# A gated encoder layer: longer split-weight tiles, with the 1024 columns placed inside them by a byte offset

## The chip, the core and the metric

The kernel runs on one core of one Trainium2 chip. The metric is the device time in microseconds of one execution. Three runs of the kernel before gave 1268.78, 1269.10 and 1269.41 us, so the median is 1269.1 us. One further execution was profiled; its own time was 1268.47 us.

## The reference

The input is `x`, 512 tokens by 1024 features, in float32, and one layer is computed:

```
x = x + 1/2 * SwiGLU_1(RMSNorm(x))                 # 1024 -> 2816 -> 1024
h = RMSNorm(x);  [A | B | gates] = h @ w_in        # 1024 -> 4608 + 1536 + 2048
A: dilated sliding-window attention, 3 groups of 8 heads of 64
B: grouped-query attention, 8 query and 2 key heads of 128, rotary
mix = (sigmoid(gA) * (oA @ P_A) + sigmoid(gB) * (oB @ P_B)) @ w_out
x = x + mix
x = x + 1/2 * SwiGLU_2(RMSNorm(x));  output RMSNorm(x)
```

## The kernel before

**Split products.** Every large product is taken in three matmuls of a reduced float32 type. Each operand is split into a high part H, rounded, and a low part L, the rest; `mm3` (L235) issues H·H, H·L and L·H into one PSUM bank (L237, L238, L239). A matmul has a stationary operand of 128x128, which TensorE loads (the PEld rows of the profile), and a moving operand of 128 rows by 512 or 256 columns, which streams past it.

**Weights.** The weights come as 288 tiles of 128x1024 float32, in one fixed list (`self.order`). A tile is loaded into a raw tile (`wr`, `wa`, `ws` or `wt`), then `prep` (L207) makes its two halves: ScalarE casts raw into `wh` (L222), VectorE subtracts to get `wl` (L223). `wh` and `wl` have three buffers each in the pool `wb`; a fourth one, with tag `whx`, lies in whichever pool `wx` is open at the time, and is used in the seven-product stages, the down projections and the `wb` projection when the tile's number n has n % 4 == 3 (L211). `ring` (L159) hands the tiles out. PE runs its instructions in the order in which the program issues them; `weights` (L227) prepares as many tiles ahead as the rings allow.

**Who reads the tiles.** A tile feeds 24 matmuls of 512 columns, or 24 of 256 columns in the seven-product stages.

- `feat` and `pair` (first FFN tiles `w13a`, `w13b`, the gates `wg`, four `waq` tiles): stationary `wh`/`wl`, moving `hH`/`hL`, 512 columns.
- `strassen` (L289): seven products for two-by-two blocks, used for most of the up projections and for the query/key projection; stationary `wh`/`wl`, moving 256 columns of `hH`/`hL`, `TH`/`TL` or `TQH`/`TQL`. A step is one tile. The stages have 14, 28 and 21 tiles in the first FFN, 35 for query/key, and 21, 28 and 21 in the second FFN: 168 in all.
- `blocks` (down projections `w2a`, `w2b`, branch products `wab`, output product `wo`): stationary `wh`/`wl`, moving `gg`, `oH`, `qH` or `mH`, 512 columns. The last three tiles of `w2b` are read twice, with 256 columns each time (L567 to L572).
- `token` (value projections `wav` of three groups, four tiles each, and `wb`, 12 tiles): here the activations `hH`/`hL` are stationary and the tile moves, 512 columns at a time. For groups 1 and 2 of `wav` the stationary operand takes every fourth token, so its 128 columns lie 16 bytes apart.

During the attention stages the gate, `waq` and `wb` work is woven in between the attention's own short matmuls and transposes, some matmuls at a time (`weave`, L365).

**Where the tiles lie.** A tile has the same byte address in each partition. The addresses follow from the tile sizes in the order in which the pools are opened, and are those of the kernel as built. What matters below is the remainder of the first byte's address by 256; slices along a tile start at multiples of 512 bytes from there, except the strided ones, which start 4, 8 or 12 bytes later.

| tile | first bytes | remainder by 256 |
|---|---|---|
| `wh`, three buffers | 50080, 54176, 58272 | 160 |
| `wl`, three buffers | 62368, 66464, 70560 | 160 |
| `whx` in the FFNs, in the query/key stage | 120352, 144928 | 32 |
| `whx` while `wb` is projected | 160160 | 160 |
| `hH0` to `hL7` | 196576 to 227296, steps of 2048 | 224 |
| `TH`, `TL`, `TQH`, `TQL` | 171744, 184032, 83424, 99808 | 224 |
| `gg`, four buffers | 136864, 145056, 153248, 161440 | 160 |
| `oH0`, `qH`, `mH0`, `kH`, `vH` | 83360, 99744, 132512, 132512, 140704 | 160 |

The lines that the change touches are in `ring` and in the mixer, where `rope_tables` (L886) opens its tables in the pool `Bp`, which then serves as `wx` for the `wb` projection.

Of the kernel before, what the change touches and what calls it, by code (L numbers as in the profile page):

```python
# [12 lines left out]
F32R = mybir.dt.float32r  # L13
# [3 lines left out]
DRAM = bass.MemoryType.DRAM  # L17

BUFS = {"wr": 3, "wa": 3, "ws": 2, "wt": 4, "wh": 3, "whx": 1}
EARLY, EARLIER = 4, 6  # L20
GROUPS = {"a": (4, 8, 16, 22), "b": (2, 8, 16, 22)}
PAIRS = ((0, 0), (1, 0), (0, 1), (0, 2), (1, 1), (1, 2), (2, 0), (3, 0), (2, 1), (2, 2), (3, 1), (3, 2))
# [16 lines left out]
NF = 22  # L39
# [26 lines left out]
def f32(t):  # L66
    return t.bitcast(F32)


class Layer:  # L70
    def __init__(self, ctx, tc, a):
# [41 lines left out]
        self.cap = len(self.order)  # L113
        self.rings = {k: [] for k in BUFS}
        self.index = {it[:2]: n for n, it in enumerate(self.order)}
# [43 lines left out]
    def ring(self, tag, n, done, last):  # L159
        held, bufs = self.rings[tag], BUFS[tag]  # L160
        pool = self.wb if tag in ("wr", "wh") else self.wx
        if pool is None or (len(held) >= bufs and held[-bufs] >= done):
            return None
        held.append(last)
        if tag[:2] != "wh":
            return pool.tile([128, 1024], F32, tag=tag, name=tag, bufs=bufs)
        return tuple(pool.tile([128, 1024], F32R, tag=t, name=t, bufs=bufs) for t in ("wh", "wl"))

    @staticmethod
    def home(it):  # L170
# [834 lines left out]
    def mixer(self):  # L1005
# [7 lines left out]
        with tc.tile_pool(name="oA", bufs=1, reuse_waits="tile") as oa:  # L1013
# [25 lines left out]
            with tc.tile_pool(name="B", bufs=1, reuse_waits="tile") as bp:  # L1039
                self.qH = bp.tile([128, 8, T], F32R, name="qH")  # L1040
                self.qL = bp.tile([128, 8, T], F32R, name="qL")
                with tc.tile_pool(name="KV", bufs=1, reuse_waits="tile") as kv:
                    self.kH = kv.tile([128, 2, T], F32R, name="kH")
                    self.kL = kv.tile([128, 2, T], F32R, name="kL")
                    self.vH = kv.tile([128, 4, 256], F32R, name="vH")
                    self.vL = kv.tile([128, 4, 256], F32R, name="vL")
                    with tc.tile_pool(name="Bp", bufs=1, reuse_waits="tile") as b2:
                        self.rope_tables(b2)
                        self.wx = b2
                        self.until(fill, ("b", 0))  # L1050
                        self.weave(self.rope_t(0, 4, 4), fill)
                        self.until(fill, ("b", 1))
                        self.weave(self.rope_t(1, 6, 6), fill)
                        self.until(fill, ("b", 2))
                        self.weave(self.rope_t(2, 6, 4), fill)
                    self.wx = None
                    with tc.tile_pool(name="Ba", bufs=2, reuse_waits="tile") as pp:
                        self.weave(self.attn_b(pp), fill)
                for _ in fill:
                    pass  # L1060
                self.hctx.close()
                with tc.tile_pool(name="M", bufs=1, reuse_waits="tile") as mp:
                    mH = [mp.tile([128, T], F32R, name=f"mH{d}") for d in range(NK)]
                    mL = [mp.tile([128, T], F32R, name=f"mL{d}") for d in range(NK)]
                    m = {}

                    def gate(j):
                        z = mp.tile([128, T], F32, tag="z", name="zg", bufs=4)
                        nc.sync.dma_start(z, self.gate_d[j])
                        nc.scalar.activation(z, z, AF.Sigmoid, bias=self.par[:, G_BG + j:G_BG + j + 1])  # L1070
                        return z

                    def done_a(d, ps):
                        m[d] = mp.tile([128, T], F32, tag="ma", name="ma", bufs=2)
                        nc.vector.tensor_mul(m[d], ps, gate(d))

                    def done_b(d, ps):
                        z = gate(NK + d)
                        nc.vector.tensor_mul(z, ps, z)
                        nc.vector.tensor_add(z, z, m[d])  # L1080
                        nc.scalar.copy(mH[d], z)
                        nc.vector.tensor_sub(mL[d], z, f32(mH[d]))

                    def done_o(d, ps):
                        nc.vector.tensor_add(self.x[d], self.x[d], ps)
                        self.norm_h(d, G_FFN2)
                        self.norm_sq(d)

                    oa_p = list(zip(self.oH, self.oL))
                    ob_p = [(self.qH[:, k, :], self.qL[:, k, :]) for k in range(8)]  # L1090
                    rows = []
                    for d in range(NK):
                        rows += [(oa_p, lambda ps, d=d: done_a(d, ps)), (ob_p, lambda ps, d=d: done_b(d, ps))]
                    self.blocks("wab", rows)
                    self.open_h()
                    mm = list(zip(mH, mL))
                    self.blocks("wo", [(mm, lambda ps, d=d: done_o(d, ps)) for d in range(NK)])
# [132 lines left out]
```

## Time and profile before

| | |
|---|---|
| median of three runs | 1269.1 us |
| profiled execution, its own time | 1268.47 us |
| span of its profile | 1266.7 us |
| PE busy | 1254.0 us, 8002 matmul records |
| PE's weight loads (PEld) busy | 1113.0 us |
| VectorE (DVE) busy | 888.2 us |
| ScalarE (ACT) busy | 587.3 us |
| bytes moved by DMA | 181.91 MB |

A matmul's recorded time runs from its start to its modelled end, and consecutive matmuls overlap. What a matmul costs the stream is the distance from its start to the next one's. A view of busy time by stretches gives it: a stretch that begins at the first matmul of a stage and ends at the first of the next, divided by the number of weight loads in it (there is one for each matmul).

### The profile page before, as it was taken

Reading aid. Unit: us, or ns where it says so; the run is one execution under the profiler, and the core shown is the slowest. Engines: PE = TensorE matmul, PEld = TensorE weight load, DVE = VectorE, ACT = ScalarE, POOL = GpSimd, SP = SyncE. Lnnn points to the kernel's source line nnn. Section 1 sums busy time; section 2 is a strip of 40 time slices with the busy share of each in tenths; the row PEclk is TensorE's granted clock in tenths of the full one; section 3 lists DMA queues with packets and bytes.
Section 4 is the critical chain, followed back from the end, with each engine's and each line's share of the span. In section 5 each row is a group of like instructions: output and inputs, shape, how many; then the busy total and the mean of one; then the engine's idle time right before and its main releaser. Section 6 shows DMA issues by size and latency. Waiting matters only on the chain.

```text
span 1266.7 us, 19954 instructions
## 1 busy us (share of the span) xinstructions
PE 1254.0 (99%) x8002; PEld 1113.0 (88%) x8002; DVE 888.2 (70%) x1339; ACT 587.3 (46%) x867; POOL 118.6 (9%) x124
## 2 busy tenths in 40 slices
PE   9999999999999999999999999999999999999997
PEld 6897999899889999877888878888889989988996
DVE  7784688478784885766557898654677847875775
ACT  8551355145453443644234465543475415532553
POOL 1111100000210212100001100000301001100001
PEclk9999999999999999999999999999999999999998
DMA  9875777342484946532232310356737536744222
GB/s 289 232 190 168 190 193 193 98 102 68 136 227 136 240 122 245 167 107 91 84 105 84 117 50 26 118 163 191 227 93 185 172 100 183 186 148 116 57 78 67
DMA packets 85549, 181.91 MB, mean 144 GB/s; under 512 B 12480, under 2 KB 19024, under 8 KB 85456
## 3 DMA queue, kind: packets, MB, share of 16 engines
q1 hardware_dynamic: 67904, 140.74, 33.6%
q0 software_dynamic: 16832, 39.34, 15.3%
q8 instruction: 63, 1.03, 0.4%
q10 hardware_dynamic: 720, 0.55, 0.1%
q14 instruction: 30, 0.25, 0.1%
HBM read 168.98 MB, written 15.29 MB: 145 GB/s over the span
## 4 chain that ended last, share of the span: by engine, by line
PE 93%; DVE 3%; issue 1%; DMA 1%; ACT 1%; POOL 0%; SPq 0%; POOLq 0%; DVEq 0%
PE mm L237 24%; PE mm L239 24%; PE mm L238 23%; PE Y L237 3%; PE Y L239 3%; PE Y L238 3%; PE X L239 2%; PE X L237 2%; PE X L238 2%; PE S L790 1%; PE mm L841 1%; PE Tb L980 1%; PE T L859 1%; DVE wl L223 0%; PE Sb L237 0%
## 5 line engine op out<-in xcount | busy, mean ns | idle before, releaser
L222 ACT CAST wh<-wr 128x1024 fp32r<-128x1024 f32 x142 | 148.9, 1049 | 211.7 <-PE mm L238 139.6
L223 DVE TENSOR_TENSOR wl<-wr,wh 128x1024 fp32r<-128x1024 f32 x142 | 173.7, 1224 | 54.8 <-ACT wh L222 54.2
L237 PE MATMUL mm<-hH,wh 128*128 128x256 f32 (+1 forms) x600 | 200.4, 334 | 0.2
L239 PE MATMUL mm<-hH,wl 128*128 128x256 f32 (+1 forms) x600 | 196.1, 327 | 0.9 <-DVE wl L223 0.9
L238 PE MATMUL mm<-hL,wh 128*128 128x256 f32 (+1 forms) x600 | 195.9, 326 | 0.3 <-DVE hL L374 0.3
L237 PE MATMUL mm<-gg,wh 128*128 128x512 f32 (+1 forms) x376 | 142.3, 379 | 0.0
L239 PE MATMUL mm<-gg,wl 128*128 128x512 f32 (+1 forms) x376 | 141.8, 377 | 0.0
L238 PE MATMUL mm<-gg,wh 128*128 128x512 f32 (+1 forms) x376 | 141.8, 377 | 0.0
L237 PEld LDWEIGHTS mm<-hH,wh 128*128 128x128 f32 x600 | 112.8, 188 | 14.9 <-issue 3.2
L239 PEld LDWEIGHTS mm<-hH,wl 128*128 128x128 f32 x600 | 112.7, 188 | 12.2 <-DVE wl L223 1.3
L238 PEld LDWEIGHTS mm<-hL,wh 128*128 128x128 f32 x600 | 112.8, 188 | 10.6 <-DVE hL L374 1.1
L222 ACT CAST wh<-wa 128x1024 fp32r<-128x1024 f32 x48 | 50.4, 1051 | 100.0 <-PE mm L238 48.6
L505 DVE TENSOR_TENSOR u<-mm,R 128x512 f32<-128x512 f32 (+1 forms) x52 | 33.7, 649 | 82.9 <-PE mm L239 82.5
L223 DVE TENSOR_TENSOR wl<-wt,wh 128x1024 fp32r<-128x1024 f32 x48 | 58.7, 1224 | 36.6 <-ACT wh L222 35.6
L238 PE MATMUL mm<-TL,wh 128*128 128x256 f32 x304 | 84.0, 276 | 0.0
L239 PE MATMUL mm<-TH,wl 128*128 128x256 f32 x304 | 84.0, 276 | 0.0
L237 PE MATMUL mm<-TH,wh 128*128 128x256 f32 x304 | 84.0, 276 | 0.0
L237 PEld LDWEIGHTS mm<-gg,wh 128*128 128x128 f32 x376 | 70.8, 188 | 14.6 <-PE mm L239 0.9
L239 PEld LDWEIGHTS mm<-gg,wl 128*128 128x128 f32 x376 | 70.8, 188 | 13.4
L222 ACT CAST wh<-ws 128x1024 fp32r<-128x1024 f32 x48 | 50.5, 1052 | 68.9 <-PE mm L238 51.4
L238 PEld LDWEIGHTS mm<-gg,wh 128*128 128x128 f32 x376 | 70.8, 188 | 13.1
L223 DVE TENSOR_TENSOR wl<-wa,wh 128x1024 fp32r<-128x1024 f32 x48 | 58.6, 1221 | 30.0 <-ACT wh L222 29.9
(233 smaller groups left out, 3164.1 us busy)
## 6 DMA issues: line engine op xcount, KB each, us to landing
wr<-in_w2a SPq DMA_DIRECT2D x22, 512.0 KB, 3.4
wr<-in_w2b SPq DMA_DIRECT2D x22, 512.0 KB, 3.9
wt<-in_w13b SPq DMA_DIRECT2D x20, 512.0 KB, 4.1
wa<-in_w13b SPq DMA_DIRECT2D x20, 512.0 KB, 3.8
wt<-in_w13b POOLq DMA_DIRECT2D x20, 512.0 KB, 5.8
wt<-in_w13a SPq DMA_DIRECT2D x18, 512.0 KB, 3.5
wt<-in_w13a POOLq DMA_DIRECT2D x18, 512.0 KB, 6.2
wa<-in_w13a SPq DMA_DIRECT2D x18, 512.0 KB, 3.4
```

The costliest lines, as they stand in the source:

```text
L222: self.nc.scalar.copy(H, raw)
L223: self.nc.vector.tensor_sub(L, raw, f32(H))
L237: mm(out, lH, rH, start=start, stop=False, skip_group_check=more)
L238: mm(out, lH, rL, start=False, stop=False, skip_group_check=more)
L239: mm(out, lL, rH, start=False, stop=stop, skip_group_check=more)
L505: nc.vector.tensor_mul(u, ps, R)
L790: nc.tensor.matmul(*args, start=True, stop=True)
L841: nc.tensor.matmul(oc, v, p, start=st, stop=sp)
L859: nc.tensor.transpose(ps[:, 128 * b:128 * b + 128], P[h][:, c0 + 128 * b:c0 + 128 * b + 128], self.ident)
L980: nc.tensor.transpose(pt[:, 128 * j:128 * j + 128], P[h, j][:, 128 * k:128 * k + 128], self.ident)
```

## The change

The tiles `wh` and `wl`, of both tags, become 1088 elements wide, which is 4352 bytes, 17 times 256. The 1024 columns in use begin `at` elements into the tile, 0 to 63, so that their first byte has the remainder that the new function `offset` names for tile n:

- seven-product stages (`sw...`): 160 for even n, 32 for odd n
- `w2a`, `wab`, `wo` and `w2b` up to its tile 18: 160
- `w2b` from its tile 19 on (those read with 256 columns): 96
- all others (`w13a`, `w13b`, `wav`, `waq` outside the seven-product stage, `wg`, `wb`): 224

`BASE` is the remainder of the tiles' own first byte: 160 in `wb`, 32 for `whx`. So that this holds for `whx` in `Bp` too, `rope_tables` gets its pool with a 128-byte tile ahead of it. All other tiles move by whole multiples of 256 bytes.

```
+BASE = {"wh": 160, "whx": 32}
...
-        return tuple(pool.tile([128, 1024], F32R, tag=t, name=t, bufs=bufs) for t in ("wh", "wl"))
+        at = (self.offset(n) - BASE[tag]) % 256 // 4
+        return tuple(pool.tile([128, 1088], F32R, tag=t, name=t, bufs=bufs)[:, at:at + 1024] for t in ("wh", "wl"))
+
+    def offset(self, n):
+        name, key = self.order[n][:2]
+        if name[:2] == "sw":
+            return 160 - 128 * (n % 2)
+        if name == "w2b" and key >= (NF + GROUPS["b"][2]) // 2:
+            return 96
+        return 160 if name in ("w2a", "w2b", "wab", "wo") else 224
...
-                        self.rope_tables(b2)
+                        self.rope_tables(self.shifted(b2, 128))
```

## The prediction

> **What bounds the kernel now.** I read the page's totals first, then the waits of PE and ScalarE, then the busy time by stretches. The page:
>
> ```profile
> span 1266.7 us, 19954 instructions
> PE 1254.0 (99%) x8002; PEld 1113.0 (88%) x8002; DVE 888.2 (70%) x1339; ACT 587.3 (46%) x867; POOL 118.6 (9%) x124
> PE 93%; DVE 3%; issue 1%; DMA 1%; ACT 1%; POOL 0%; SPq 0%; POOLq 0%; DVEq 0%
> ```
>
> PE is busy for 1254.0 of 1266.7 us and holds 93% of the chain that ended last. Who waits for whom (engine, line, releaser; total us, times, longest):
>
> ```profile
> PE warm L1106 <- POOL R L94: 1.3, 1, 1.3
> PE rb L406 <- POOL r L391: 1.0, 1, 1.0
> PE mm L239 <- DVE wl L223: 0.9, 1, 0.9
> ACT wh L222 <- PE mm L238: 277.1, 123, 5.5
> ```
>
> The preparation of the weights waits for PE to free a buffer (277.1 us in 123 waits), and PE waited only once for a weight half, 0.9 us. So what a matmul takes off the stream comes off the time, and the question is how many nanoseconds each matmul takes. The stretches below begin and end at the first matmuls of tiles or stages; the columns are the stretch, its length, then busy us and instructions of PE and PEld.
>
> ```profile
> core 0: us, PE busy (x) PEld busy (x) DVE busy (x) ACT busy (x) POOL busy (x), PEclk, DMA share, GB/s
> 31.57:53.54 21.97, 21.97 (x98) 18.03 (x96) 16.98 (x22) 11.74 (x17) 3.65 (x3) 1.00 0.98 284
> 53.54:73.33 19.79, 19.79 (x169) 19.79 (x168) 14.63 (x14) 9.81 (x12) 3.58 (x3) 1.00 0.72 159
> 73.33:92.37 19.04, 19.04 (x170) 19.04 (x169) 16.17 (x17) 10.77 (x12) 1.20 (x1) 1.00 0.66 193
> 242.36:247.95 5.59, 5.59 (x26) 4.53 (x24) 2.52 (x3) 1.06 (x2) 0.00 (x0) 1.00 0.32 98
> 247.95:258.84 10.89, 10.89 (x49) 9.01 (x48) 6.26 (x7) 2.09 (x3) 1.18 (x1) 1.00 0.37 83
> 373.34:396.21 22.87, 22.87 (x98) 22.82 (x97) 6.24 (x7) 5.59 (x6) 0.31 (x1) 1.00 0.40 115
> 639.20:661.60 22.40, 22.40 (x97) 18.05 (x96) 15.65 (x55) 8.39 (x14) 1.41 (x2) 1.00 0.31 106
> 874.67:918.19 43.52, 43.52 (x194) 36.05 (x192) 26.65 (x29) 18.20 (x24) 12.58 (x9) 1.00 0.80 238
> 1237.39:1245.98 8.59, 8.59 (x73) 8.58 (x72) 5.86 (x11) 4.07 (x8) 1.95 (x2) 1.00 0.00 0
> ```
>
> PE is never idle in them and the granted clock is 1.00, yet the same shape of matmul has several prices. With 512 columns: 43.52/192 = 226.7 ns in `wo`, and 10.89/48 = 226.9 in two `w2a` tiles in `wh`; 21.97/96 = 228.9 in `feat`; 5.59/24 = 232.9 in a `w2a` tile that lies in `whx`; 22.40/96 = 233.3 in `token` on `wb`; 22.87/96 = 238.2 on the strided `wav` group. With 256 columns: 19.04/168 = 113.3, 19.79/168 = 117.8, and 8.59/72 = 119.3 at the end. 113.3 is half of 226.7; I take both as the floor of the stream.
>
> Put beside the table of addresses, the 512-column prices sort by d, the remainder of the operand to be loaded less that of the moving one. d = 0 (`wo`, `w2a` in `wh`) gives the floor; d = 192 (160 against 224, `feat`) 2.2 ns over it; d = 128 (32 against 160) 6.2; d = 64 (224 against 160, `token`) 6.7. That 256 is the period is seen in `gg` and `mH`: their addresses differ by 256 modulo 512, and both stand at the floor. The groups of instructions in such stretches say the same with recorded times, which are some 162 ns longer than the distance between starts (the first row from 874.7 to 918.1, the second from 242.4 to 247.9, the third from 639.3 to 661.5):
>
> ```profile
> L237 PE MATMUL mm<-mH,wh 128*128 128x512 f32 x64 | 24.9, 389 | 0.0
> L237 PE MATMUL mm<-gg,wh 128*128 128x512 f32 x8 | 3.2, 396 | 0.0
> L237 PE MATMUL mm<-wh,hH 128*128 128x512 f32 x32 | 12.7, 396 | 0.0
> ```
>
> **The change, term by term.** Nothing is issued that was not issued before, but for the byte position of operands. The casts and subtractions keep their 1024 columns; if another offset made each pair 0.1 us longer, it would lie in the 277.1 us for which ScalarE waits anyway (uncovered, 288 tiles would be 29 us). The 128-byte tile in `Bp` moves the rotary tables and 40 short transposes; cost zero.
>
> *(a) `w2a`/`w2b` tiles in `whx`, d from 128 to 0.* n % 4 == 3 falls on 11 of the tiles read with 512 columns: 11 x 24 x (232.9 - 226.9) = 1.58 us. I take 1.5. Bounds 0 and 1.6.
>
> *(b) `token` on contiguous columns, d from 64 to 0.* `wb` has 12 tiles, the first `wav` group 4: 16 x 24 x (233.3 - 226.7) = 2.5 us. Rotary transposes lie between some of them, and after an interruption the stream does not come back to the floor at once (see d), so I take 2.0. Bounds 0.8 and 2.5.
>
> *(c) `feat` in the FFNs, d from 192 to 0.* 8 + 4 tiles: 12 x 24 x 2.2 = 0.63 us; I take 0.5, bounds 0 and 0.6. The first eight tiles run while DMA is at a share of 0.98, so 0.3 of this could be given back as a wait for a weight half.
>
> *(d) `feat` woven into attention, 20 tiles, d from 192 to 0.* Here three to twelve matmuls run between transposes. The groups from 709 to 809.3, where `Sb` has d = 0 already and `feat` has d = 192:
>
> ```profile
> L237 PE MATMUL mm<-hH,wh 128*128 128x512 f32 x56 | 22.4, 399 | 0.0
> L239 PE MATMUL mm<-hH,wl 128*128 128x512 f32 x56 | 22.0, 393 | 0.0
> L238 PE MATMUL mm<-hL,wh 128*128 128x512 f32 x56 | 21.9, 391 | 0.0
> L237 PE MATMUL Sb<-kH,qH 128*128 128x512 f32 x32 | 12.8, 400 | 0.0
> L239 PE MATMUL Sb<-kH,qL 128*128 128x512 f32 x32 | 12.6, 394 | 0.0
> L238 PE MATMUL Sb<-kL,qH 128*128 128x512 f32 x32 | 12.5, 392 | 0.0
> ```
>
> Equal remainders buy nothing in so short a run: means of 395 (`Sb`) and 394 (`feat`), against 389 in the steady stretch. I take 0. Bounds: 480 x 3 ns = 1.4 us lost, if `feat` becomes like the slower `Sb` rows, and 480 x 5 = 2.4 gained, if it reaches 389.
>
> *(e) `token` on strided columns, two `wav` groups, 8 tiles, d from 64..76 to 0..12.* No row has a strided load near d = 0. The loads' recorded time in 373.4 to 396.1 (strided) and 349.1 to 373.3 (contiguous):
>
> ```profile
> L238 PEld LDWEIGHTS mm<-wl,hH 128*128 128x128 f32 x32 | 9.9, 310 | 0.0
> L238 PEld LDWEIGHTS mm<-wl,hH 128*128 128x128 f32 x32 | 6.0, 188 | 1.3
> ```
>
> The strided load is 122 ns longer, so it may itself set the 238.2 ns, and then the offset changes nothing; that is the nearest row, and I take 0. Bounds: 192 x (238.2 - 226.7) = 2.2 us gained; as much lost as (b) wins per matmul, 192 x 6.7 = 1.3.
>
> *(f) Seven-product stages, 168 tiles, 256 columns.* The moving remainder stays 224; the tiles' goes from 160, 160, 160, 32 to 160 and 32 in turn. The stages, and the second one again without its first tile:
>
> ```profile
> 53.54:92.37 38.83, 38.83 (x337) 38.83 (x336) 30.80 (x31) 20.58 (x24) 4.78 (x4) 1.00 0.69 175
> 138.69:214.96 76.27, 76.27 (x673) 76.26 (x672) 62.33 (x62) 41.65 (x47) 8.33 (x7) 1.00 0.75 192
> 141.52:214.96 73.44, 73.44 (x650) 73.44 (x649) 59.81 (x59) 40.62 (x46) 8.33 (x7) 1.00 0.74 194
> 258.84:316.07 57.23, 57.23 (x505) 57.23 (x504) 44.06 (x44) 30.94 (x35) 1.19 (x1) 1.00 0.31 86
> 396.21:491.63 95.42, 95.42 (x842) 95.42 (x840) 77.08 (x83) 44.05 (x50) 13.36 (x15) 1.00 0.64 182
> 941.54:999.42 57.88, 57.88 (x506) 57.87 (x505) 47.45 (x49) 31.44 (x36) 7.26 (x6) 1.00 0.73 188
> 1043.29:1119.67 76.38, 76.38 (x674) 76.37 (x672) 62.34 (x62) 41.65 (x47) 8.43 (x7) 1.00 0.72 189
> 1163.55:1220.88 57.33, 57.33 (x505) 57.33 (x504) 44.05 (x44) 30.92 (x35) 1.20 (x1) 1.00 0.30 86
> ```
>
> There are two states, 117.8 and 113.3 ns, at both remainders. A stage starts in the slow one and falls into the fast one where the remainder jumps from 160 to 32: the second stage is fast from its second tile on (73.44/648 = 113.3), the first one only from its eighth, at its second jump (53.54 to 73.33 slow, then fast). Once fast, it stays fast across every later jump. The stages' lengths over 113.33 ns for each of their 336, 672, 504, 840, 504, 672 and 504 matmuls are 0.75, 0.11, 0.11, 0.22, 0.76, 0.22 and 0.21 us, together 2.4, which is 22 slow tiles of 24 x 4.5 = 0.107 us. With a jump at every tile I expect one to three slow tiles per stage, some 10, and so 12 x 0.107 = 1.3 us. Bounds: 0 and 2.4; the loss is the last rival.
>
> *(g) The last three `w2b` tiles, 144 matmuls of 256 columns, d from 0, 0 and 128 to 192.* 119.3 ns becomes 117.8 or 113.3, as in (f); there is no jump here, so I take the slow one: 0.2 us. Bounds 0 and 0.86.
>
> Sum: 1.5 + 2.0 + 0.5 + 0 + 0 + 1.3 + 0.2 = 5.5 us. The span would be 1261.2; the profiled execution, 1.77 us longer than its span, 1263.0; the median of the runs shown lies 0.63 over the profiled one, so **1263.6 us**.
>
> One rule of the skill speaks against all of this. The Trainium skill, TensorE: Matmul & The Clock Gate, Part 2, step by step, says that PE has two independent read ports, and that loading the next weights takes no read bandwidth from the running matmul; by it no term above exists and the time stays at 1269.1. The trace does not agree: it has rows of 389 and 396 ns for one shape at one clock.
>
> **The rivals.** A difference of 0.2%, 2.5 us, is about what a measurement of this kernel can tell.
>
> 1. *Equal remainders help only in steady streams.* The `Sb` rows speak for it, `wo` and `w2a` say nothing of it. (d) costs 1.4, (b) falls to 1.0, (e) costs 0.5, some third of its bound: 5.5 - 1.4 - 1.0 - 0.5 = 2.6, so 1266.5 us. Chance 0.20.
> 2. *The prices belong to something other than the remainder*, such as the pool or which operand moves, since in this kernel each reader has its own remainder. Then nothing changes: 1269.1 us. Against it: `gg` has two prices in one stage with one reader. Chance 0.08. This is the case in which the page named above would be right.
> 3. *The floor everywhere.* All upper bounds together are 1.6 + 2.5 + 0.6 + 2.4 + 2.2 + 2.4 + 0.9 = 12.6; with (d) and (e) at half, 10.3, so 1258.8 us; 9 to 10 is the likelier part. Chance 0.13.
> 4. *Slower: a jump at every tile keeps the seven-product stages slow.* In the first stage the first jump to 32 and the jump back left 117.8 standing. If every jump sets the stream back, 146 more tiles are slow: 15.6 us lost against 4.2 gained elsewhere, 1280.5 us. It decides from 39 more slow tiles on, 61 of 168. Against it: 648 matmuls at 113.3 with a jump to 32 and back at every fourth tile. Chance 0.05.
>
> **How the numbers follow.** The forecast, 4.2 to 7 us gained, has 0.54, with a range of its own of 1262.1 to 1264.9. The range of 1259.0 to 1267.6 takes in the first rival and most of the third, and leaves out the second, the fourth and the third's end, less than 0.2. Faster by over 0.2%: the forecast, the third rival and half of the first, 0.78; within 0.2%: the second, half of the first, rounded, 0.17; slower 0.05.
>
> **What would show it.** In the profile of the changed kernel: (a) no `gg` group with 512 columns over 390 ns; (b) `wb` and the first `wav` group near 389 to 391 instead of 396; (c) `feat` in the FFNs at 389 in all three rows; (d) `feat` rows between attention's within 3 ns of now; (e) the strided rows still near 400; (f) 256-column rows at 276 from the second or third tile of each stage; (g) the end at 280. The forecast is wrong if PE's idle time grows by over 1 us, if the steady `token` and `feat` stretches keep their prices at d = 0, or if 280 spreads through the seven-product stages.

## The result and the profile after

The changed kernel took 1262.25 us (median of four runs, 1261.51 to 1262.37) where the kernel before took 1269.1 (1268.78 to 1269.41). The ratio is 0.9945, with a 95% interval of 0.9928 to 0.9962. A second series, of the same changed kernel under the name after_again, gave 1262.23 us beside 1268.69, ratio 0.9952, interval 0.9940 to 0.9965. The profiled execution of the changed kernel took 1262.37 us, 1.77 more than its span, as before.

In the changed kernel's file the lines of the products stand ten lower: `mm3` issues at L247, L248 and L249, the cast is L232, the subtraction L233. The page's totals and PE's and ScalarE's waits:

```profile
span 1260.6 us, 19952 instructions
PE 1246.3 (99%) x8002; PEld 1109.8 (88%) x8002; DVE 886.8 (70%) x1339; ACT 587.2 (47%) x867; POOL 119.1 (9%) x124
PE mm L851 <- DVE PT L871: 1.5, 1, 1.5
PE mm L249 <- DVE wl L233: 1.0, 1, 1.0
PE stat L408 <- DVE acc L591: 0.9, 1, 0.9
ACT wh L232 <- PE mm L248: 272.2, 123, 5.3
```

The span fell by 6.1 us and PE's busy time by 7.7; the 1.6 between them are new idle time of PE (12.7 us before, 14.3 after). Most of it is the first row: the wait for `PT`, the transposed probabilities of the dilated attention, was 0.5 us before and is 1.5 now. The wait for `acc`, near the end, went from 0.6 to 0.9. The row of the wait for `PT` in the kernel before:

```profile
PE mm L841 <- DVE PT L861: 0.5, 1, 0.5
```

Busy time by stretches, of the changed kernel, each from the first matmul of a stage to the first of the next (columns as in the prediction): the first seven-product stage, the second `w2a`, `wav` group 0, group 1, the query/key stage, group 2, the dilated attention, `wb`, the second attention, and the first three passes over `w2b`'s last tiles.

```profile
53.10:91.31 38.21, 38.21 (x338) 38.20 (x336) 30.76 (x31) 20.56 (x24) 4.78 (x4) 1.00 0.69 179
213.61:257.15 43.54, 43.54 (x194) 36.05 (x193) 23.16 (x27) 9.90 (x11) 1.18 (x1) 1.00 0.35 105
347.04:370.78 23.74, 23.74 (x113) 19.58 (x112) 22.26 (x36) 16.99 (x22) 4.79 (x4) 1.00 0.85 236
370.78:393.34 22.56, 22.56 (x97) 22.52 (x97) 6.27 (x7) 5.57 (x6) 0.00 (x0) 1.00 0.41 116
393.34:488.55 95.21, 95.21 (x842) 95.20 (x840) 77.07 (x83) 44.06 (x50) 13.36 (x15) 1.00 0.63 183
488.55:516.77 28.22, 28.22 (x151) 26.08 (x149) 10.71 (x43) 13.57 (x38) 9.37 (x17) 1.00 0.84 272
516.77:636.67 119.90, 118.41 (x846) 92.86 (x844) 76.00 (x247) 49.27 (x134) 2.67 (x5) 1.00 0.34 104
636.67:705.02 68.35, 68.35 (x313) 56.30 (x312) 51.22 (x125) 29.31 (x46) 9.37 (x10) 1.00 0.28 97
705.02:805.32 100.30, 99.59 (x506) 81.69 (x504) 86.83 (x171) 56.10 (x117) 2.14 (x2) 1.00 0.15 53
1231.72:1240.20 8.48, 8.48 (x73) 8.48 (x72) 5.80 (x11) 4.01 (x9) 2.03 (x2) 1.00 0.00 0
```

The same stages in the kernel before, where the prediction did not show them (second `w2a`, `wav` group 0, group 2, dilated attention, `wb`, second attention):

```profile
214.96:258.84 43.88, 43.88 (x194) 36.09 (x193) 23.13 (x27) 9.91 (x11) 1.18 (x1) 1.00 0.36 105
349.07:373.34 24.27, 24.27 (x114) 19.59 (x112) 22.39 (x36) 17.03 (x22) 4.48 (x4) 1.00 0.83 230
491.63:520.08 28.45, 28.45 (x150) 26.27 (x149) 10.71 (x43) 13.60 (x38) 9.36 (x17) 1.00 0.82 270
520.08:639.20 119.12, 118.62 (x845) 92.85 (x844) 76.00 (x247) 49.38 (x134) 2.67 (x5) 1.00 0.34 105
639.20:709.00 69.80, 69.80 (x313) 56.37 (x312) 51.43 (x125) 29.32 (x46) 9.36 (x10) 1.00 0.29 95
709.00:809.37 100.37, 99.77 (x505) 81.70 (x504) 86.77 (x171) 56.17 (x117) 2.14 (x2) 1.00 0.15 53
```

Every stage with a steady stream became shorter or stayed; one stage became longer, the dilated attention, by 0.78 us. Taking the differences of all stages and sorting them by the prediction's terms:

| term | predicted gain, us | measured | where |
|---|---|---|---|
| (a) `w2a`, `w2b`, `whx` tiles | 1.5 | 1.79 | six stages, 0.17 to 0.34 each |
| (b) `token`, contiguous | 2.0 | 1.97 | group 0 of `wav` 0.53, `wb` 1.44 |
| (c) `feat` in the FFNs | 0.5 | 0.62 | 0.18 and 0.19, and 0.25 among the first loads |
| (d) `feat` in attention | 0 | -0.70 | dilated -0.78, second attention 0.08 |
| (e) `token`, strided | 0 | 0.55 | 0.31 and 0.24 |
| (f) seven-product stages | 1.3 | 1.45 | 0.63, 0, 0, 0.21, 0.63, -0.01, -0.01 |
| (g) last `w2b` tiles | 0.2 | 0.39 | |
| sum | 5.5 | 6.1 | |

The 0.25 in (c) lie where the first tiles are still arriving; that stretch, from the span's start to the first matmul of the third tile, was 17.94 us before and 17.69 after, and between 17.25 and 17.98 in the profiles of the runs below, so they say nothing of the change.

The groups of the same stretches (the first row from 213.61 to 257.15, then one from 636.67 to 658.8, one from 370.78 to 393.34, and two from 705.02 to 805.32):

```profile
L247 PE MATMUL mm<-gg,wh 128*128 128x512 f32 x64 | 24.9, 389 | 0.0
L247 PE MATMUL mm<-wh,hH 128*128 128x512 f32 x33 | 12.8, 389 | 0.0
L247 PE MATMUL mm<-wh,hH 128*128 128x512 f32 x32 | 12.7, 398 | 0.0
L247 PE MATMUL mm<-hH,wh 128*128 128x512 f32 x56 | 22.3, 398 | 0.0
L247 PE MATMUL Sb<-kH,qH 128*128 128x512 f32 x32 | 12.7, 398 | 0.0
```

`gg` and `wb` stand at 389 ns, the row of the floor; the strided `token` (third row) does not, nor does `feat` woven into attention (fourth), which was 399 before.

### The profile page after: what moved, and what is told of

Its sections match the earlier page's. It is cut to its first block, busy times and chain, and to the rows that moved or that the text cites. A ratio compares the mean times of both kernels' runs of the same rounds, so it can differ in the third digit from the quotient of the medians.

```text
span 1260.6 us, 19952 instructions
## 1 busy us (share of the span) xinstructions
PE 1246.3 (99%) x8002; PEld 1109.8 (88%) x8002; DVE 886.8 (70%) x1339; ACT 587.2 (47%) x867; POOL 119.1 (9%) x124
## 4 chain that ended last, share of the span: by engine, by line
PE 93%; DVE 2%; DMA 1%; ACT 1%; issue 1%; SPq 0%; POOLq 0%; POOL 0%; DVEq 0%
PE mm L247 24%; PE mm L249 24%; PE mm L248 24%; PE Y L247 3%; PE Y L248 3%; PE Y L249 3%; PE X L247 2%; PE X L248 2%; PE X L249 2%; PE mm L851 1%; PE Tb L990 1%; PE S L800 1%; PE T L869 1%; DMA d<-SO 1%; PE Sb L247 0%
## 5 line engine op out<-in xcount | busy, mean ns | idle before, releaser
L232 ACT CAST wh<-wr 128x1024 fp32r<-128x1024 f32 x142 | 148.9, 1049 | 212.3 <-PE mm L248 136.4
L233 DVE TENSOR_TENSOR wl<-wr,wh 128x1024 fp32r<-128x1024 f32 x142 | 173.3, 1221 | 53.9 <-ACT wh L232 53.4
L247 PE MATMUL mm<-hH,wh 128*128 128x256 f32 (+1 forms) x600 | 199.4, 332 | 0.3 <-ACT hH L383 0.3
L249 PE MATMUL mm<-hH,wl 128*128 128x256 f32 (+1 forms) x600 | 195.6, 326 | 1.0 <-DVE wl L233 1.0
L248 PE MATMUL mm<-hL,wh 128*128 128x256 f32 (+1 forms) x600 | 195.5, 326 | 0.3 <-DVE hL L384 0.3
L247 PE MATMUL mm<-gg,wh 128*128 128x512 f32 (+1 forms) x376 | 141.5, 376 | 0.0
L248 PE MATMUL mm<-gg,wh 128*128 128x512 f32 (+1 forms) x376 | 141.1, 375 | 0.0
L249 PE MATMUL mm<-gg,wl 128*128 128x512 f32 (+1 forms) x376 | 141.0, 375 | 0.0
L247 PEld LDWEIGHTS mm<-hH,wh 128*128 128x128 f32 x600 | 112.7, 188 | 14.8 <-issue 3.2
L249 PEld LDWEIGHTS mm<-hH,wl 128*128 128x128 f32 x600 | 112.7, 188 | 12.0 <-DVE wl L233 1.4
L248 PEld LDWEIGHTS mm<-hL,wh 128*128 128x128 f32 x600 | 112.7, 188 | 10.4 <-DVE hL L384 1.2
L232 ACT CAST wh<-wa 128x1024 fp32r<-128x1024 f32 x48 | 50.5, 1051 | 98.4 <-PE mm L248 48.2
L233 DVE TENSOR_TENSOR wl<-wt,wh 128x1024 fp32r<-128x1024 f32 x48 | 58.7, 1224 | 36.0 <-ACT wh L232 35.1
L247 PE MATMUL mm<-TH,wh 128*128 128x256 f32 x304 | 83.9, 276 | 0.0
L248 PE MATMUL mm<-TL,wh 128*128 128x256 f32 x304 | 83.9, 276 | 0.0
L249 PE MATMUL mm<-TH,wl 128*128 128x256 f32 x304 | 83.9, 276 | 0.0
L247 PEld LDWEIGHTS mm<-gg,wh 128*128 128x128 f32 x376 | 70.6, 188 | 14.0 <-PE mm L249 0.9
L232 ACT CAST wh<-ws 128x1024 fp32r<-128x1024 f32 x48 | 50.5, 1053 | 68.0 <-PE mm L248 50.7
L249 PEld LDWEIGHTS mm<-gg,wl 128*128 128x128 f32 x376 | 70.6, 188 | 12.9
L248 PEld LDWEIGHTS mm<-gg,wh 128*128 128x128 f32 x376 | 70.6, 188 | 12.5
L233 DVE TENSOR_TENSOR wl<-wa,wh 128x1024 fp32r<-128x1024 f32 x48 | 58.6, 1220 | 29.3 <-ACT wh L232 29.2
```

What stands on the lines that cost most here:

```text
L232: self.nc.scalar.copy(H, raw)
L233: self.nc.vector.tensor_sub(L, raw, f32(H))
L247: mm(out, lH, rH, start=start, stop=False, skip_group_check=more)
L248: mm(out, lH, rL, start=False, stop=False, skip_group_check=more)
L249: mm(out, lL, rH, start=False, stop=stop, skip_group_check=more)
```

## The experiments

The theory: what a matmul of this kind costs the stream depends on where its two operands begin modulo 256 bytes, and with 256 columns also on a jump of that position. The rivals: the price belongs to the tile's buffer or width (the prediction's second rival), or the jump does harm (its fourth).

**Longer tiles in their old positions** (long_only). `offset` returns zero extra elements, and the rotary tables stay where they were.

```
-        at = (self.offset(n) - BASE[tag]) % 256 // 4
+        at = self.offset(n)
...
+        return 0
...
-                        self.rope_tables(self.shifted(b2, 128))
+                        self.rope_tables(b2)
```

> Tiles 1088 elements wide, but the columns begin where they began before (160 in the pool wb and in the wb projection, 32 in whx of the other pools). If the remainder by 256 alone sets the price: no stage of steady matmuls moves by more than 0.1 us and the time is 1269.1 within 1.5. If the longer slots or the shifted pools do it (other addresses modulo 512 and 1024): 1262 to 1263.

It took 1268.91 us (1268.11 to 1269.58) beside 1268.53, ratio 1.0004, interval 0.9994 to 1.0013. Its first two seven-product stages, `wb`, and the first stage of the second FFN:

```profile
53.40:92.23 38.83, 38.83 (x337) 38.83 (x336) 30.53 (x31) 20.31 (x24) 4.78 (x4) 1.00 0.67 175
138.56:214.82 76.26, 76.26 (x673) 76.26 (x672) 62.34 (x62) 41.65 (x47) 8.33 (x7) 1.00 0.73 193
639.10:708.90 69.80, 69.80 (x314) 56.37 (x313) 51.45 (x125) 29.32 (x46) 9.36 (x10) 1.00 0.28 95
941.42:999.29 57.87, 57.87 (x506) 57.87 (x504) 47.35 (x49) 31.41 (x36) 7.26 (x6) 1.00 0.71 185
```

They are those of the kernel before to 0.01 us. The wider tiles and the new distances between buffers do nothing; what the change gains lies in the positions inside 256 bytes. The 128-byte tile ahead of the rotary tables, which this run leaves out, was not tried alone.

**No jump** (no_jump). All tiles of the seven-product stages at 160.

```
-            return 160 - 128 * (n % 2)
+            return 160
```

> The changed kernel with all seven-product tiles at 160, moving operands at 224. If only a jump of the remainder brings the 256-column stream from 117.8 to 113.3 ns: nearly all 168 tiles at 117.8, stages longer by 160 x 24 x 4.5 ns = 17 us in sum, 1279 us; recorded matmuls of 280 instead of 276 ns. If the stream falls into the fast state by itself and the alternation is decoration: 1262 to 1264.

One execution took 1279.05 us. Its second seven-product stage and its query/key stage:

```profile
138.63:217.78 79.15, 79.15 (x673) 79.14 (x672) 62.29 (x62) 41.34 (x47) 8.33 (x7) 1.00 0.71 186
399.68:498.61 98.93, 98.93 (x842) 98.93 (x840) 77.73 (x83) 44.05 (x50) 13.67 (x15) 1.00 0.62 176
```

79.15/672 and 98.93/840 are 117.8 ns: the higher price from end to end, 2.9 and 3.5 us longer than the kernel before. The jump does not disturb these stages, it is what makes them fast, and the kernel before had it by chance of its fourth buffer.

**Maps of the positions** (map, map2). Each tile of `wab` and `wo` gets a different remainder, so that d changes while stage, reader and buffers stay; the strided `wav` tiles too; each seven-product stage gets one pattern. Of map (in the first line, which is for the seven-product stages, `first` is the number of the stage's first tile and `odd` is n % 2; strided tiles at 0, 32, 64, 96, 128 and 192):

```
...
+            return {8: 32, 30: 160, 66: 224, 101: 96, 196: (96, 224)[odd], 225: (160, 224)[odd], 261: 160 if n == first else 32}[first]
+        if name == "wo":
+            return (160 + 32 * key) % 256
+        if name == "wab":
+            return (160 + 16 * key) % 256
...
```

> One look at many remainders, the rest as in the changed kernel. wo, eight tiles, 512 columns, moving at 160, tiles at 160 and on in steps of 32: by d alone 226.7 ns at d = 0, 233 at 64 and 128, 229 at 192, the steps of 32 between them unknown; if the pool or the reader sets the price, 226.7 for all. wab, twelve tiles in steps of 16: a slope between. Seven-product stages, moving at 224: all at 32, all at 160 (slow throughout, 117.8, if a jump is needed), all at 224 (d = 0: 120 as at the end of the kernel before, or 113.3 as 512 columns would suggest), all at 96 (d = 128: 118), 96 and 224 in turn, 160 and 224 in turn (unknown), and one jump from 160 to 32 after the first tile (113.3 from the second or third tile on, if one jump is enough). Strided wav: tiles at 0, 32, 64, 96, 128, 192: 238 at all of them if the strided load itself is the limit, else a spread of over 3 ns. The last three w2b tiles at 96, 224, 96: 113.3 after the first jump if a jump does it there too, a gain of 0.3 us on the changed kernel.

One execution took 1282.48 us. Six tiles of 24 matmuls each in the branch products and `wo` (d = 0, 16 and 32 at 818 to 835; d = 0, 32 and 224 later):

```profile
818.17:823.61 5.44, 5.44 (x25) 4.50 (x24) 2.33 (x4) 2.83 (x5) 0.00 (x0) 1.00 0.70 197
823.61:829.06 5.45, 5.45 (x25) 4.50 (x24) 3.32 (x5) 4.46 (x7) 0.00 (x0) 1.00 0.81 287
829.06:834.65 5.59, 5.59 (x25) 4.51 (x24) 2.15 (x3) 2.45 (x4) 0.00 (x0) 1.00 0.53 188
884.93:890.39 5.46, 5.46 (x25) 4.51 (x24) 3.12 (x4) 1.64 (x2) 1.27 (x1) 1.00 0.77 220
890.39:895.98 5.59, 5.59 (x25) 4.51 (x24) 2.58 (x3) 2.20 (x3) 0.00 (x0) 1.00 1.00 266
923.90:929.50 5.60, 5.60 (x25) 4.50 (x24) 3.18 (x4) 2.20 (x3) 0.00 (x0) 1.00 0.27 94
```

5.44/24 is 226.7 ns and 5.60/24 is 233.3. Tile by tile from the starts of the matmuls, `wo` gave 227.5 at d = 0, 233.0 at 32, 233.4 at 64, 233.7 at 96, 233.4 at 128, 233.5 at 160, 229.4 at 192 and 233.3 at 224. One reader in one stage thus has the prices that the kernel before had spread over its readers of contiguous operands, at a granted clock of 1.00, and so the prediction's second rival falls. The load on the DMA engines does not sort these prices either: the tile at 5.60 us above ran beside a DMA share of 0.27, the first one at 5.44 beside 0.70. The Trainium skill, TensorE: Matmul & The Clock Gate, Part 2, step by step, says that loading the next weights takes no read bandwidth from the running matmul; by that rule these tiles would all cost the same. They differ by 7 ns in 227, so the measurement goes against the rule as far as this float type and these shapes go. Whether the two reads get in each other's way, and how, no run here shows.

With 256 columns the floor is another matter. In map, a stage with all tiles at 224, d = 0, ran at 120.0 ns, as slow as any. The rows below are from map: three tiles at 224, 160 and 224 in turn, then a stage with one jump, its first tile at 160 and the twenty others at 32.

```profile
1056.30:1059.17 2.87, 2.87 (x25) 2.86 (x24) 2.52 (x3) 1.03 (x1) 0.00 (x0) 1.00 0.34 61
1059.17:1061.89 2.72, 2.72 (x26) 2.72 (x25) 1.23 (x1) 1.54 (x2) 0.00 (x0) 1.00 0.55 187
1061.89:1064.77 2.88, 2.88 (x26) 2.88 (x25) 1.23 (x1) 1.53 (x2) 0.00 (x0) 1.00 0.55 192
1178.24:1181.07 2.83, 2.83 (x26) 2.83 (x25) 2.52 (x3) 1.02 (x1) 0.00 (x0) 1.00 0.38 68
1181.07:1235.47 54.40, 54.40 (x483) 54.40 (x482) 41.56 (x41) 29.98 (x34) 1.20 (x1) 1.00 0.29 88
```

The stage with one jump runs at 54.40/480 = 113.3 ns after it: one jump suffices.

map2 asked for the direction of the jump, for positions close to d = 0 and for finer strided ones.

```
...
+            return {8: 128, 30: 32 if n == first else 160, 66: 0, 101: (160, 32)[odd], 196: (0, 128)[odd], 225: 160 if n < 235 else 32, 261: (192, 64)[odd]}[first]
+        if name == "wo":
+            return (160 + (240, 8, 24, 244, 248, 252, 4, 12)[key]) % 256
...
```

> A second look at remainders, the rest as in the changed kernel. wo, moving at 160: d = -16, 8, 24, -12, -8, -4, 4, 12; the first map had 226.7 at 0, 227.0 at 16, 233 at 32 and 224: I expect 227 up to 16 on both sides and a step to 230 or more at 24. Seven-product stages: d = 160 and d = 32 throughout (118 to 120, no jump), one jump from 32 to 160 after the first tile (113.3 if the direction does not matter, 117.8 if it does), 32 first and then 160 in turn with it, 0 and 128 in turn, ten tiles at 160 and then 32 to the end (117.8 until the jump and 113.3 behind it, if the jump alone does it), 192 and 64 in turn. Strided wav at 48 to 80: 233 to 235. gates woven into attention back at 160: 0.1 to 0.2 us longer in each attention stage.

One execution took 1277.10 us. The rows: the second seven-product stage (first tile at 32, all others at 160); the sixth (ten tiles at 160, the rest at 32) before its jump and after it; two tiles of `wo`, at d = 248 and 252.

```profile
139.04:218.20 79.16, 79.16 (x674) 79.16 (x672) 62.57 (x62) 41.51 (x47) 8.33 (x7) 1.00 0.72 187
1049.83:1078.10 28.27, 28.27 (x242) 28.27 (x241) 19.45 (x19) 14.31 (x17) 2.41 (x2) 1.00 0.64 170
1078.10:1127.06 48.96, 48.96 (x435) 48.96 (x434) 42.57 (x44) 26.95 (x30) 6.05 (x5) 1.00 0.72 193
900.88:906.48 5.60, 5.60 (x26) 4.51 (x25) 3.82 (x3) 2.20 (x3) 2.78 (x3) 1.00 1.09 294
906.48:911.92 5.44, 5.44 (x25) 4.50 (x24) 2.58 (x3) 2.20 (x3) 1.79 (x1) 1.00 0.73 235
```

A jump from 32 to 160 leaves the stage slow to its end (79.16/672 = 117.8); one from 160 to 32 makes it fast at once (28.27/240 = 117.8, then 48.96/432 = 113.3). Not every jump from 160 to 32 does it: in the kernel before, the first one in the first stage of each FFN left 117.8 standing. Close to equal remainders the map is not smooth, and this went against what I expected: d = 252 is at the floor, d = 244 and 248 at 233, d = 4 at 232, d = 8 at 231. Nor is d all there is to it. d = 16 cost 227.0 ns right behind a tile with d = 0 (in map) and 233.2 right behind the attention (in map2), and d = 228 and 240 stood at the floor behind tiles with d = 0. The stream seems to keep a state; only d = 0 was at or near the floor in every steady stretch of 512 columns with contiguous operands.

Of the strided tiles, those at 64 cost 233.3 to 233.5 ns, at 48 233.5, those at 224 (as in the change) 235.0, and those at 0, 32, 56, 68, 72, 80, 96, 128 and 192 between 235.4 and some 240. None came near 226.7.

**The best positions put together** (best1, best2, best3). Seven-product stages of the second FFN begin at 160 instead of 32 where the count made them begin at 32; the strided tiles stand at 64; the last `w2b` tiles at 96, 224, 96.

```
-            return 160 - 128 * (n % 2)
+            return 160 - 128 * ((n - (0 if name[2] != "b" or n < 217 else 1)) % 2)
...
-            return 96
+            return 224 if key == 20 else 96
+        if name == "wav" and key >= 4:
+            return 64
```

> Offsets as the first map suggests: every seven-product stage but the query/key one starts at 160 and goes on at 32 in turn (saves one slow tile, 0.107 us, in each of the last two stages); the two strided wav groups at 64 (233.3 instead of 235.0 ns, 0.3 us); the last three w2b tiles at 96, 224, 96 (0.2 us). Against the changed kernel 0.7 us less, 1261.5 by the median shown. If these prices hang on what runs before a stage, and not on the offsets, the stages stand where the changed kernel has them, 1262.2.

> As the variant with other offsets, and the gap of woven matmuls ahead of the first two value steps of the dilated attention is 10 instead of 8. If PE's wait there (0.5 to 1.6 us) is for the softmax sums' round trip through DRAM, two more groups of three matmuls (1.4 us) take most of it away: 0.5 to 1.4 us less than the variant without it. If the wait has another cause it stays, and the time too.

best1 took 1261.45 us (1260.98 to 1261.98) beside 1268.69, ratio 0.9946, interval 0.9933 to 0.9960. It gained 0.11 us in each of the last two seven-product stages, 0.23 in the passes over the last `w2b` tiles and 0.26 in the strided groups, as the maps had it, but lost 0.20 in the query/key stage: behind tiles at 64 that stage began with two slow tiles, where behind tiles at 224 it had been fast from its first. That was not expected. best2 has in addition `GAP_1 = 10` in place of 8, so that two more steps of woven work come ahead of the first `values_a` of the dilated attention; it took 1261.03 us (1260.88 to 1261.24) beside 1268.69, ratio 0.9941, interval 0.9929 to 0.9954, the lowest median of all. That is 0.42 us below best1, a little less than the 0.5 that was expected at least.

best3 puts the last value tile ahead of the query/key stage back to 224:

```
-            return 64
+            return 224 if key == 7 else 64
```

> As best2, but the last value tile ahead of the query/key stage (key 7) stands at 224 again and not at 64. Theory: which state a seven-product stage begins in hangs on the remainder of the matmuls ahead of it, and the query/key stage, fast at once after tiles at 224 and slow for two tiles after tiles at 64, is fast at once: 0.20 us less in that stage, against at most 0.04 more in the value tile, 1260.9. Rival: it hangs on the state that the whole value stage has left behind, or on time; one tile changes nothing and the query/key stage stays at 95.42: 1261.0 to 1261.1.

It took 1261.13 us (1260.66 to 1262.18) beside 1268.58, ratio 0.9942, interval 0.9930 to 0.9955. Its query/key stage is 95.42 us long, as in best2:

```profile
393.23:488.65 95.42, 95.42 (x842) 95.42 (x840) 77.09 (x83) 44.05 (x50) 13.35 (x15) 1.00 0.63 182
```

My theory missed, though the test was a narrow one: `token` reads the last two value tiles in turn, six matmuls each, so only the last six matmuls ahead of the stage stood at 224 and the six before them at 64, and the stage began slow. Nor is 224 needed: in map2, where both tiles stood at 68, the stage began with 113.9 ns and then 113.3. What decides the state in which a stage begins stays open.

**The wait in the dilated attention** (gap10, before_gap10). The same one line, `GAP_1 = 10`, alone in the changed kernel and alone in the kernel before.

```
-GAP_1 = 8
+GAP_1 = 10
```

> The changed kernel with one line more changed: GAP_1 from 8 to 10, so two more steps of gate and value matmuls are woven in before the first values_a of the dilated attention. Theory: the 0.78 us that this stage lost is PE's one wait for PT, which is late because the softmax sums come back late from DRAM; two more steps of 0.2 to 0.25 us ahead of it take most of the 1.3 to 1.5 us wait, so that this stage, the wb projection and the second attention together (288.55 us in the changed kernel, 289.29 before) come to 287.9 to 288.1, and the time to 1261.6 to 1261.8. Rival: the woven feat matmuls themselves became dearer at equal remainders; then the three stages stay at 288.4 to 288.6 and the time at 1262.2.

> The kernel before with GAP_1 at 10 and nothing else. It says how much of the gain of GAP_1 belongs to the change. Theory: the wait for PT was 0.5 us there, so at most 0.5 us is to be had: 1268.2 to 1268.6 beside 1268.7. Rival: the weaving order is better by itself, whatever the remainders: as much gain as in the changed kernel, 0.6 us or more, 1268.1 or less.

A step is three matmuls, some 0.7 us, and not the 0.2 to 0.25 us of the first of these expectations. gap10 took 1261.38 us (1261.24 to 1262.20) beside 1268.58, ratio 0.9944, interval 0.9932 to 0.9957, which does not set it apart from the changed kernel, and its median lies a little under the range expected; before_gap10 took 1268.29 (1267.16 to 1268.82), ratio 0.9996, interval 0.9987 to 1.0005. Since the gap moves work between neighbouring stages, the three stages from the dilated attention to the second attention are taken together: 289.29 us before, 288.55 after, 287.87 in gap10, 289.35 in before_gap10. PE's wait for `PT` in gap10:

```profile
PE mm L851 <- DVE PT L871: 0.3, 1, 0.3
```

Why it exists is seen in the timeline of SP, which stores the softmax sums to DRAM and reads them back, shifted, when the stores have landed, in two round trips (start, us of issue; here the first one). In the kernel before:

```profile
529.68 1.37 SPq L813 DMA_DIRECT2D d<-SO  x2
533.92 0.33 SPq L815 DMA_DIRECT2D SO<-d  x1
```

The same two in the changed kernel:

```profile
526.50 1.10 SPq L823 DMA_DIRECT2D d<-SO  x2
531.36 0.33 SPq L825 DMA_DIRECT2D SO<-d  x1
```

And in gap10:

```profile
526.45 1.44 SPq L823 DMA_DIRECT2D d<-SO  x2
531.39 0.33 SPq L825 DMA_DIRECT2D SO<-d  x1
```

From the second store to the reading back it is 4.24 us before, 4.86 after and 4.94 in gap10. The store of the second round trip stands behind this on SP's queue, and the scaling, the transposes and `PT` behind them. The second reading back, in the kernel before and in the changed one:

```profile
542.35 0.37 SPq L816 DMA_DIRECT2D SO<-d  x1
539.99 0.37 SPq L826 DMA_DIRECT2D SO<-d  x1
```

Counted from the stage's first matmul (520.08 and 516.77) that is 22.27 us before and 23.22 after, 0.95 later. PE does not come to the wait any earlier: it is there 30.74 us after that matmul in the kernel before and 30.69 in the changed one. In the eight profiles with the gap of 8 the wait follows the second reading back: 0.50 us at 22.27 and 0.54 at 22.31 (long_only), 0.82 at 22.56 (no_jump), 0.89 at 22.62 (best1), 0.97 at 22.69 (map2), 1.26 at 22.98 (after_again), 1.49 at 23.22 and 1.57 at 23.30 (map). It is the sums that came back later, and how late they come varies by 0.74 us among the six of these profiles with other positions than before, by 0.24 between the two of the changed kernel itself; in before_gap10, with the old positions, it was 22.93. Why the stores land later is not settled, nor how much of it comes from the change.

In gap10 PE has more work ahead of the wait, and the second reading back stood at 22.79: the wait falls from 1.5 to 0.3 us and the three stages by 0.68 us, to which the 0.43 us by which the sums came back earlier may have added. In the kernel before the same line is worth nothing in these stages. With the wait covered the three stages gain 1.48 us by the change (289.35 against 287.87), where the first profile of the changed kernel gained 0.74; with the gap of 8 the same three stages took 288.34 us in after_again and 287.94 in no_jump, so what the wait takes of the gain differs from profile to profile.

> The changed kernel once more, timed beside the two variants of it. If the 0.8 us that the woven attention stage lost in its profile is the landing time of the small DMAs that carry the softmax sums through DRAM, it differs from execution to execution: the wait of PE for the copy of PT between 0.5 and 1.6 us here, all other stages within 0.05 us of the first profile. If it comes from the change, 1.5 us again.

after_again, whose result stands at the top, had the same lengths as the first profile to 0.02 us in all stages but two, the stretch of the first loads (17.77 us) and the dilated attention, 119.67 with a wait of 1.3 us for `PT`. That lies between the two readings of its expectation and does not decide between them.

## Why the prediction was right

Its 1263.6 us is 1.35 over the 1262.25 measured. 0.6 of that are the terms, 6.1 us against 5.5; 0.75 is the step from the profiled execution to the median, where I added 0.63 us as before, while the profiled execution of the changed kernel lies 0.12 over its median. The 0.63 us belonged to that one series: in the later ones the kernel before has medians of 1268.53 to 1268.69.

- **What bounds it.** That what a matmul takes off the stream comes off the time held: ScalarE still waits 272.2 us for PE, and PE's wait for a weight half went from 0.9 to 1.0 us.
- **(a)** 1.79 us, over my upper bound of 1.58. In the second `w2a` stage the length over 192 matmuls at 226.67 ns fell from 0.36 us (43.88) to 0.02 (43.54). Two tiles in `whx` at 6.2 ns a matmul are 0.30 of that; the rest lay in the tiles in `wh`, whose 226.9 I had taken for their floor. The mechanism was right, the term a little small.
- **(b)** 1.97 against 2.0. The prediction's discount for the rotary transposes was right in size: `wb` went by 1.44 us, where twelve tiles at the full difference would have given 1.9.
- **(c)** 0.37 in the stretches that can be read, 0.5 predicted. In `w13b` it is the whole term (96 x 2.2 ns = 0.21, measured 0.19); in `w13a` the 144 matmuls behind the first loads should have gained 0.32 and gained 0.18, and PE's wait for a weight half there grew by 0.1, the loss that the prediction had allowed for.
- **(d)** is the step that failed. The matmuls themselves did nearly as predicted: 399 ns became 398, `Sb` beside them 398, and PE's busy time fell by 0.21 us in the dilated attention (118.62 to 118.41) and by 0.18 in the second (99.77 to 99.59). But "I take 0" left out that PE waits in this stage for the softmax sums' round trips through DRAM. Of 0.78 us lost, the wait for `PT` is 1.0: PE came to it no earlier, and the sums came back 0.95 us later. Whether the change made them late or that profile did is not shown. The prediction named PE's idle time growing by over 1 us as a sign that the forecast is wrong. It grew by 1.6, and the forecast stood only because the other terms, measured, came to 6.8: (a), (e) and (g) gave 1.0 us more than forecast, (d) took 0.7, and that these nearly cancel is luck.
- **(e)** 0 predicted, 0.55 measured. The strided load does not set the price alone, as I had taken from its longer record: with the offset it went from 238.2 to 235.0 ns, and to 233.3 at 64. Nor does it reach the floor at any of the positions tried. The bounds held.
- **(f)** 1.45 against 1.3. The lengths over 113.33 ns come to 0.92 us, 8.6 slow tiles where I expected some 10. That the fall from slow to fast is made by a jump from 160 to 32 is shown by no_jump, map and map2. Why two such jumps were needed in the first stage of each FFN of the kernel before stays open, and so does the query/key stage's quick start.
- **(g)** 0.39 against 0.2: 8.48/72 = 117.8 ns, the price predicted, but down from 119.3, is 0.11 of it; the other 0.28 came in the three passes that follow, which the prediction had not looked at by themselves.

Of the rivals, the first (only steady streams gain) falls with (b), which gained its 1.97 us among interruptions, and with PE's busy time in the two attention stages, which fell by 0.39 us where this rival had 1.4 lost. The second falls with long_only and map. The third, the floor everywhere, fails in attention, in the strided groups and at the end. The fourth has its sign turned round: 146 tiles kept slow is what comes without a jump, and the 15.6 us that it gave for them is near what no_jump lost against the changed kernel (1279.05 - 1262.25 = 16.8).

## What to carry to other kernels

Where PE is the bound and one shape of matmul shows several recorded times at one granted clock, group the rows by the remainder of the operands' first bytes before looking for anything else, and try positions, since a few hundred bytes of padding cost nothing here. Take such a map per shape: what was best with 512 columns (equal remainders) was worst with 256. After the change, compare the waits of the bound engine one by one with those before. Where one grew, look whether the engine came to it earlier or what it waits for came later, and in several profiles, since a round trip through DRAM varied here by up to 1.0 us; work woven in ahead of such a wait covered most of it.

## What the runs showed of the hardware that was not expected

- With 512 columns the price of a 128x128 by 512 matmul follows the two operands' positions modulo 256, from 226.7 ns at d = 0 to 235.0 at d = 28, but not d alone: 226.7 ns also at d = 228 and 240 behind a tile at d = 0, 227.0 and 233.2 for one d (16) in two runs, and 233 at d = 244 and 248 beside 227.0 at 252.
- With 256 columns there are more than two prices: 113.3 ns; 117.8 for tiles at 160 alone or at 32 alone; 118.3 at 0; 118.6 at 96; 120.0 at 128 and at 224, where d = 0. The release works from 160 to 32, though not at each such jump, and not from 32 to 160, and it holds across later jumps between the two. With 160 and 224 in turn, each tile has its own price, 113.3 and 120.0.
- The small stores of the softmax sums took 4.2 to 4.9 us from the second one's issue to the reading back, in kernels that differ in nothing of that chain but the addresses.
